# The ratio of group A's two softmax sums: from ScalarE and VectorE to VectorE alone

## The chip, the cores and the metric

The kernel runs on one core of one Trainium2 chip. The metric is the device time of one launch in microseconds. The kernel before has a median of 923.14 us over 3 runs (922.13 to 925.34).

## The reference

Two layers of a transformer trunk work on 512 latent tokens (an 8 x 64 grid) and 256 context tokens, model width 1024. Each layer makes one adaLN-modulated norm, one input projection to 3584 columns, three groups of attention heads (A, B, C), a SiLU gate on each, one output projection and a gated residual. The change lies in group A, differential attention with 4 heads of two softmaxes each:

```python
s = jnp.einsum('bqhmd,bkhmd->bhmqk', q, k).astype(jnp.float32) * (q.shape[-1] ** -0.5)
p = jax.nn.softmax(s, axis=-1)
a = (p[:, :, 0] - lam * p[:, :, 1]).astype(v.dtype)
return jnp.einsum('bhqk,bkhd->bqhd', a, v)
```

Latent queries attend to 512 latent and 256 context keys in one softmax; context queries (in layer 0 only) attend to the 256 context keys. The result of each head is RMS-normalised, so a common factor of a row does not matter much until that norm. Group B is grouped-query attention, group C attention in a neighbourhood of the grid with a bias table.

## The kernel before, in words

**Products.** A projection in float32 is made of three matmuls of rounded parts (high x high, high x low, low x high; lines 679 to 681, tile `proj`). Weights stream in through SyncE's DMA queue (line 76, `raw`); ScalarE casts each piece to its high part (line 89, `whi`) and VectorE or GpSimd makes the low part (line 92, `wlo`). The results leave PSUM tile by tile: norms and rotary embedding for queries and keys (lines 462 to 534, through ScalarE, VectorE and GpSimd, then a transposing DMA), a scaled split for values (lines 585 and 586), a tanh gate (lines 600 to 606).

**Attention.** A unit is 128 queries and one pair of softmaxes in group A (16 latent units in each layer, 8 context units in layer 0), or one head in groups B and C. Five steps follow one another:

- `stage_S`: TensorE makes the scores (line 775, tile `sc`, two PSUM buffers).
- `stage_M`: VectorE takes the row maximum (line 830; in group C line 827 with the bias table), ScalarE turns it into the bias of the exponential (line 832).
- `stage_E`: ScalarE takes the exponential (line 844) into a float32 tile `p` (tag `p32`, three buffers) and, in group A, also its row sum into `dn`. A latent unit of group A does S, M and E twice, once for each softmax.
- `stage_H`: for group A the two exponentials become one matrix, p0 + k p1, where k = -lambda sum0 / sum1 (lines 857 to 860). Then ScalarE casts it to float16 (line 864, tile `hl`), GpSimd (for a few of the units in group C VectorE) subtracts to get the rest (line 865), and a transposing DMA on SyncE's queue brings both into `pt` (line 867).
- `stage_PV`: TensorE multiplies `pt` with the values (lines 900 and 901, tile `pv`), and for every fourth unit of group A `pv_evac` normalises and gates the result (lines 911 to 929).

Step H runs one unit behind the scores, step PV four units behind. Since the tile `p` has three buffers and a latent unit of A uses two, the second exponential of a unit waits until line 860 of the unit before has read the first.

**Stages.** Each layer runs A, then B, then C. Beside the attention of each stage TensorE works through filler: the projections for the next group (during A those of B and a gate, during B those of C and a gate), and during C the output projection (`op` at lines 1087 to 1089; in layer 1 also `oh` and `ot`, lines 1141 to 1143) and the transposes of the attention's result (`yt`, lines 618 and 640). Before group C's first scores a bias table is loaded (line 985, into `stB`, the buffer that held B's queries and keys) and scaled by ScalarE (line 987).

**What sets the order.** The code is written unit by unit, but a scheduler orders the instructions of each engine when the program is built, by priorities and by its own estimates of the durations. So a change of one instruction can move others on every engine, and in later stages. Each engine then works through its own list strictly in that order: an instruction that waits holds up everything behind it on its engine.

**The lines that the change touches.** In `stage_H` line 857 (ScalarE) makes m = -lambda sum0, line 858 (VectorE) makes 1/sum1, line 859 (ScalarE) makes k = m/sum1, and line 860 (VectorE) the combination p0 + k p1 over 128 x 768 (context units 128 x 256). All of m, k and the sums are columns of 128 x 1 in `dn`. There are 40 units, so 40 of each.

Of the kernel before, what the change touches and what calls it, by code (L numbers as in the profile page):

```python
# [15 lines left out]
AF = mybir.ActivationFunctionType  # L16
ALU = mybir.AluOpType
# [99 lines left out]
def tile_hybrid_block(ctx: ExitStack, tc: tile.TileContext, xT_d, cT_d, ng_d, w_ada, bT_d, w_in, w_out,  # L117
# [7 lines left out]
    V, A, G, PE, SP = nc.vector, nc.scalar, nc.gpsimd, nc.tensor, nc.sync  # L125
# [3 lines left out]
    def sb(shape, dt=F32, tag="", bufs=1):  # L129
        return pool.tile(shape, dt, tag=tag, bufs=bufs, name=tag)  # L130
# [169 lines left out]
    lc = {}  # L300
# [547 lines left out]
    def stage_H(l, u, lo_eng):  # L848
        hl = sb([128, 1536], F16, "hl", 4)
        if u["g"] == "A":  # L850
            n, h = u["w"], u["segs"][0] // 2
            den = acc["dn", u["j"]]
            p0 = u["p", 0][:, 0:n]
            p = u["p", 1][:, 0:n] if u["lat"] else u["p", 0][:, n:2 * n]
            k = den[:, 1, 4 + h:5 + h]
            m = den[:, 0, 4 + h:5 + h]
            A.activation(out=m, in_=den[:, 0, h:h + 1], func=AF.Copy, scale=lc[l]["nlam"])
            V.reciprocal(k, den[:, 1, h:h + 1])
            A.activation(out=k, in_=k, func=AF.Copy, scale=m)
            V.scalar_tensor_tensor(out=p, in0=p, scalar=k, in1=p0, op0=ALU.mult, op1=ALU.add)  # L860
        else:
            n = u["w"] * len(u["segs"])
            p = u["p", 0][:, 0:n]
        A.copy(out=hl[:, 0:n], in_=p)  # L864
        lo_eng.tensor_tensor(out=hl[:, n:2 * n], in0=p, in1=hl[:, 0:n], op=ALU.subtract)  # L865
        pt = sb([128, 12, 128], F16, "pt", 4)
        SP.dma_start_transpose(out=pt[:, 0:n // 64, :], in_=hl[:, 0:2 * n])  # L867
        u["pt"] = pt
# [106 lines left out]
    def attn(l, g):  # L975
# [15 lines left out]
        for x in range(n + LAG):  # L991
# [25 lines left out]
            if HLAG <= x < n + HLAG:  # L1017
                stage_H(l, us[x - HLAG], share("H"))
# [341 lines left out]
```

## Time and profile before

| | |
|---|---|
| median of 3 runs | 923.14 us (922.13 to 925.34) |
| profiled execution, its own time | 924.36 us |
| its span in the trace | 922.5 us (1.86 us lie around it) |
| mean granted clock of TensorE | 0.952 |
| stage A of layer 0 (scores of A from 108 us on) | about 112 to 270 us |
| stage A of layer 1 | about 630 to 735 us |
| stage C of layer 1 and the end | about 825 to 922.5 us |

How to read it: the stage limits are taken from where the first and last instructions of a stage start, and stages overlap by a few microseconds. Busy time of an engine in a stretch is the time in which it has an instruction under way; the rest is a wait for another engine, a DMA or its own sequencer. Idle time of an engine other than the one that bounds a stage costs nothing by itself.

### The profile page before, as it was taken

Reading aid. Unit: us, or ns where it says so; the run is one execution under the profiler, and the core shown is the slowest. Engines: PE = TensorE matmul, PEld = TensorE weight load, DVE = VectorE, ACT = ScalarE, POOL = GpSimd, SP = SyncE. Lnnn points to the kernel's source line nnn. Section 1 sums busy time; section 2 is a strip of 40 time slices with the busy share of each in tenths; the row PEclk is TensorE's granted clock in tenths of the full one; section 3 lists DMA queues with packets and bytes.
Section 4 is the critical chain, followed back from the end, with each engine's and each line's share of the span. In section 5 each row is a group of like instructions: output and inputs, shape, how many; then the busy total and the mean of one; then the engine's idle time right before and its main releaser. Section 6 shows DMA issues by size and latency. Waiting matters only on the chain. (4 is left out here: it accounts for less than half of the span.)

```text
span 922.5 us, 17964 instructions
## 1 busy us (share of the span) xinstructions
PE 825.3 (89%) x6386; PEld 706.9 (77%) x6386; DVE 679.0 (74%) x1306; ACT 592.4 (64%) x1269; POOL 541.3 (59%) x502
## 2 busy tenths in 40 slices
PE   5898997996998899897999989989959999988988
PEld 3787876895987789785778889879849878865767
DVE  5985787988678866558656797789877967656843
ACT  5334577784887687477653445478758988839830
POOL 2638855899698565435330047938988886634420
PEclk9899999998999999898999989989969999997989
DMA  9834895645979996998898713784557899996642
GB/s 328 306 97 126 202 214 141 139 95 134 193 162 222 202 223 173 219 259 215 184 211 237 258 52 101 185 185 102 133 128 175 149 190 246 231 260 171 152 91 83
DMA packets 307049, 165.46 MB, mean 179 GB/s; under 512 B 256528, under 2 KB 275216, under 8 KB 306704
## 3 DMA queue, kind: packets, MB, share of 16 engines
q1 hardware_dynamic: 306960, 164.33, 73.7%
q8 instruction: 50, 0.82, 0.4%
q14 instruction: 39, 0.32, 0.1%
HBM read 86.55 MB, written 15.47 MB: 111 GB/s over the span
## 5 line engine op out<-in xcount | busy, mean ns | idle before, releaser
L865 POOL TENSOR_TENSOR hl<-p,hl 128x768 f16<-128x768 f32 (+3 forms) x138 | 203.6, 1480 | 164.9 <-ACT hl L864 148.8
L679 PE MATMUL proj<-whi,bigL 128*128 128x384 f32 (+1 forms) x592 | 203.0, 344 | 8.4 <-DVE tb L602 4.2
L680 PE MATMUL proj<-wlo,bigL 128*128 128x384 f32 (+1 forms) x592 | 199.4, 337 | 0.8 <-POOL wlo L92 0.7
L681 PE MATMUL proj<-whi,bigL 128*128 128x384 f32 (+1 forms) x592 | 197.3, 335 | 0.0
L844 ACT ACTIVATE p<-sc,nb,gsc 128x768 f32<-128x768 f32 (+3 forms) x200 | 166.4, 846 | 10.6 <-DVE p L860 4.7
L830 DVE TENSOR_REDUCE mx<-sc 128x1 f32<-128x768 f32 (+2 forms) x128 | 118.7, 932 | 33.2 <-PE sc L775 33.0
L679 PEld LDWEIGHTS proj<-whi,bigL 128*128 128x128 f32 x592 | 115.2, 195 | 18.7 <-DVE tb L602 5.9
L864 ACT CAST hl<-p 128x768 f16<-128x768 f32 (+3 forms) x144 | 104.1, 726 | 38.5 <-DMA pt<-hl 22.5
L680 PEld LDWEIGHTS proj<-wlo,bigL 128*128 128x128 f32 x592 | 115.5, 195 | 3.9 <-POOL wlo L92 1.5
L681 PEld LDWEIGHTS proj<-whi,bigL 128*128 128x128 f32 x592 | 114.6, 194 | 2.8 <-issue 2.0
L92 POOL TENSOR_TENSOR wlo<-raw,whi 128x768 fp32r<-128x768 f32 (+1 forms) x44 | 83.4, 1902 | 40.3 <-ACT whi L89 37.5
L89 ACT CAST whi<-raw 128x768 fp32r<-128x768 f32 (+1 forms) x104 | 80.3, 780 | 28.4 <-DMA raw<-in_w_in_dram 14.0
L900 PEld LDWEIGHTS <-pt 128*128 128x128 f16 x736 | 65.5, 99 | 35.3 <-DMA pt<-hl 20.9
L679 PE MATMUL proj<-whi,bigC 128*128 128x384 f32 (+2 forms) x224 | 76.0, 339 | 1.0 <-ACT xn L462 1.0
L92 DVE TENSOR_TENSOR wlo<-raw,whi 128x768 fp32r<-128x768 f32 (+1 forms) x60 | 64.9, 1085 | 15.9 <-ACT whi L89 14.4
L680 PE MATMUL proj<-wlo,bigC 128*128 128x384 f32 (+2 forms) x224 | 74.8, 334 | 0.0
L163 POOL TENSOR_TENSOR rsqb<-rsqb,half 128x12 f32<-128x12 f32 (+2 forms) x25 | 68.4, 2737 | 10.0 <-DVE rsqb L162 9.2
L681 PE MATMUL proj<-whi,bigC 128*128 128x384 f32 (+2 forms) x224 | 74.1, 333 | 0.0
L901 PEld LDWEIGHTS <-pt 128*128 128x128 f16 x736 | 66.0, 100 | 4.3 <-issue 2.2
L832 ACT ACTIVATE nb<-mx,lnp,gsc 128x1 f32<-128x1 f32 (+1 forms) x104 | 39.7, 386 | 36.5 <-DVE mx L830 24.4
L775 PE MATMUL sc<-bigL 128*128 128x512 f16 (+4 forms) x184 | 46.4, 312 | 18.0 <-ACT p L844 17.2
L900 PE MATMUL pv<-vA,pt 128*128 128x128 f16 (+2 forms) x424 | 51.3, 228 | 9.6 <-DMA pt<-hl 9.2
(320 smaller groups left out, 2031.5 us busy)
## 6 DMA issues: line engine op xcount, KB each, us to landing
raw<-in_w_in_dram SPq DMA_DIRECT2D x64, 384.0 KB, 4.0
adw<-in_w_ada_dram SPq DMA_DIRECT2D x68, 256.0 KB, 3.6
raw<-in_w_out_dram SPq DMA_DIRECT2D x16, 384.0 KB, 4.7
raw<-in_w_in_dram SPq DMA_DIRECT2D x16, 256.0 KB, 3.1
g_d<-tb SPq DMA_DIRECT2D x20, 192.0 KB, 2.7
gt<-g_d SPq DMA_DIRECT2D x18, 192.0 KB, 3.4
hl<-in_w_ada_dram SPq DMA_DIRECT2D x12, 256.0 KB, 5.2
pt<-in_w_ada_dram SPq DMA_DIRECT2D x12, 256.0 KB, 5.2
```

The costliest lines, as they stand in the source:

```text
L89: self.nc.scalar.copy(out=hi, in_=raw2)
L92: self.share("W").tensor_tensor(out=lo, in0=raw2, in1=hi.bitcast(F32), op=ALU.subtract)
L163: G.tensor_tensor(out=y, in0=x, in1=half[:, 0:n], op=ALU.pow)
L679: PE.matmul(ps, lhsT=xh, rhs=hi, start=(kt == 0), stop=False)
L680: PE.matmul(ps, lhsT=xh, rhs=lo, start=False, stop=False)
L681: PE.matmul(ps, lhsT=xl, rhs=hi, start=False, stop=(kt == KT - 1))
L830: V.tensor_reduce(out=mx[:, 0:ns], in_=ps[:, 0:w * ns].rearrange("p (a b) -> p a b", b=w), axis=AX.X, op=ALU.max)
L844: A.activation(out=p[:, w * x:w * x + w], in_=u["ps", i][:, w * x:w * x + w], func=AF.Exp, bias=u["nb", i][:, x:x + 1], scale=lc[l]["sc"][ ...
L864: A.copy(out=hl[:, 0:n], in_=p)
L865: lo_eng.tensor_tensor(out=hl[:, n:2 * n], in0=p, in1=hl[:, 0:n], op=ALU.subtract)
L900: PE.matmul(po[r, :], lhsT=pt[:, b, r], rhs=V_[:, vt, c0:129], start=first, stop=False)
L901: PE.matmul(po[r, 0:65 - c0], lhsT=pt[:, nb + b, r], rhs=V_[:, vt, c0:65], start=False, stop=stop)
```

## The change

The ratio is made by VectorE alone: the reciprocal of the second sum as before, and then one product of two factors, (1/sum1) x (-lambda) x sum0, in one instruction. ScalarE's two instructions for each unit go, and the column m is no longer written.

```diff
             k = den[:, 1, 4 + h:5 + h]
-            m = den[:, 0, 4 + h:5 + h]
-            A.activation(out=m, in_=den[:, 0, h:h + 1], func=AF.Copy, scale=lc[l]["nlam"])
             V.reciprocal(k, den[:, 1, h:h + 1])
-            A.activation(out=k, in_=k, func=AF.Copy, scale=m)
+            V.scalar_tensor_tensor(out=k, in0=k, scalar=lc[l]["nlam"], in1=den[:, 0, h:h + 1], op0=ALU.mult,
+                                   op1=ALU.mult)
             V.scalar_tensor_tensor(out=p, in0=p, scalar=k, in1=p0, op0=ALU.mult, op1=ALU.add)
```

In the changed kernel the lines from the reciprocal on have numbers one lower: the reciprocal is line 856, the new product 857 and the combination 859, the cast 863, the bias table's load 984.

The scheduler makes a new order from this. On VectorE, for the first unit of stage A in layer 0, the old order has two other instructions between the reciprocal and the combination:

```order
206 L246 COPY adt<-ada 128x128
207 L858 RECIPROCAL dn<-dn 128x1
208 L506 TENSOR_TENSOR stg<-xn,stg 128x16x32
209 L830 TENSOR_REDUCE mx<-sc 128x1
210 L860 SCALAR_TENSOR_TENSOR p_1679<-p_1679,dn,p_1669 128x768
211 L602 SCALAR_TENSOR_TENSOR tb<-sq,proj 128x256
```

In the new order, at the same place on VectorE, the reciprocal, the new product (`dn<-dn,lm`) and the combination stand together:

```order
206 L246 COPY adt<-ada 128x128
207 L856 RECIPROCAL dn<-dn 128x1
208 L857 SCALAR_TENSOR_TENSOR dn<-dn,lm 128x1
209 L859 SCALAR_TENSOR_TENSOR p_1679<-p_1679,dn,p_1669 128x768
210 L506 TENSOR_TENSOR stg<-xn,stg 128x16x32
211 L830 TENSOR_REDUCE mx<-sc 128x1
```

So the combination moved ahead of a split for the keys (line 506) and ahead of the next row maximum (line 830). On ScalarE, at the same unit, the old order is:

```order
103 L832 ACTIVATE nb<-mx,lm,gsc 128x1
104 L857 ACTIVATE dn<-dn,lm 128x1
105 L844 ACTIVATE p_1679,dn<-sc,nb,gsc 128x768
106 L505 CAST stg<-xn 128x16x32
107 L859 ACTIVATE dn<-dn 128x1
108 L600 ACTIVATE sq<-proj 128x256
109 L832 ACTIVATE nb<-mx,lm,gsc 128x1
110 L844 ACTIVATE p_1706,dn<-sc,nb,gsc 128x768
111 L864 CAST hl<-p_1679 128x768
```

and the new one:

```order
103 L832 ACTIVATE nb<-mx,lm,gsc 128x1
104 L844 ACTIVATE p_1679,dn<-sc,nb,gsc 128x768
105 L505 CAST stg<-xn 128x16x32
106 L600 ACTIVATE sq<-proj 128x256
107 L863 CAST hl<-p_1679 128x768
108 L832 ACTIVATE nb<-mx,lm,gsc 128x1
109 L844 ACTIVATE p_1706,dn<-sc,nb,gsc 128x768
```

Here the cast of the combined matrix moved ahead of the next unit's exponential. Later stages change as well. On SyncE's queue in layer 1, around the load of group C's bias table (`stB<-in_btab_dram`), the old order is:

```order
411 L867 DMA_TRANSPOSE pt<-hl 128x12x128
412 L606 DMA g_d_82<-tb 128x384
413 L867 DMA_TRANSPOSE pt<-hl 128x12x128
414 L606 DMA g_d_82<-tb 128x384
415 L867 DMA_TRANSPOSE pt<-hl 128x12x128
416 L606 DMA g_d_82<-tb 128x384
417 L985 DMA stB<-in_btab_dram 128x2944
418 L76 DMA raw<-in_w_out_dram 128x512
```

and the new one:

```order
394 L971 DMA gt<-g_d_82 128x384
395 L866 DMA_TRANSPOSE pt<-hl 128x12x128 x2
396 L1098 DMA bigC<-x_d 128x1024
397 L866 DMA_TRANSPOSE pt<-hl 128x12x128
398 L984 DMA stB<-in_btab_dram 128x2944
399 L866 DMA_TRANSPOSE pt<-hl 128x12x128
400 L638 DMA xn<-o_d_80 128x256 x3
```

The table's load now stands ahead of B's last transposing DMA and no longer behind three stores of gates (line 606). Counted over TensorE's whole order, the products of filler (matmuls of `proj`, `op`, `oh`, `ot`) that stand between the scores are these:

| filler products on TensorE | before | changed |
|---|---|---|
| layer 0, first to last score of A | 610 | 634 |
| layer 1, first to last score of A | 489 | 434 |
| layer 1, B's last score to C's first score | 18 | 75 |
| layer 1, C's first to last score | 173 | 97 |
| layer 1, behind the last score | 151 | 209 |

## The prediction

> **What bounds the kernel now.** I read the engines' busy shares first, then the busy time by stage, then the waits in the two A stages, and last the groups by line. The page's shares:
>
> ```profile
> PE 825.3 (89%) x6386; PEld 706.9 (77%) x6386; DVE 679.0 (74%) x1306; ACT 592.4 (64%) x1269; POOL 541.3 (59%) x502
> ```
>
> TensorE (PE) is busy for 825.3 of 922.5 us, and the change takes no work from it. It can only pay where TensorE is idle, 97 us in all. The busy time by stage, for the two A stages (columns: stretch, length, then busy us of PE, PEld, DVE, ACT, POOL, the granted clock, DMA share, GB/s):
>
> ```profile
> 112.00:270.00 158.00, 139.17 (x1080) 121.81 (x1079) 133.32 (x221) 121.92 (x308) 122.54 (x126) 0.97 0.69 155
> 630.00:735.00 105.00, 91.39 (x633) 81.78 (x632) 89.61 (x122) 82.53 (x182) 92.25 (x82) 0.92 0.61 136
> ```
>
> TensorE idles 158.0 - 139.2 = 18.8 us and 105.0 - 91.4 = 13.6 us there, 32.4 us together. No engine is far ahead: VectorE (DVE) has 84% and 85%, ScalarE (ACT) 77% and 79%, GpSimd (POOL) 78% and 88%. What TensorE waits for, first in 112 to 270, then in 630 to 735 us (total, times, longest):
>
> ```profile
> PE sc L775 <- ACT p L844: 10.0, 6, 3.3
> PE pv L900 <- DMA pt<-hl: 3.8, 5, 1.9
> ...
> PE sc L775 <- ACT p L844: 5.2, 3, 3.9
> PE pv L900 <- DMA pt<-hl: 4.6, 2, 3.0
> ```
>
> Scores wait for an exponential to free their PSUM buffer for 10.0 + 5.2 = 15.2 us, and the value products for the transposed matrix for 8.4 us. Both hang on the chain exponential, ratio, combination, cast, transposing DMA, so the ratio lies on a path that TensorE waits for, some of the time. Its instructions and their neighbours, by group (count | busy us, mean ns | idle before and releaser):
>
> ```profile
> L844 ACT ACTIVATE p<-sc,nb,gsc 128x768 f32<-128x768 f32 x112 | 110.8, 989 | 8.8 <-DVE p L860 4.5 <-DVE vnb L546 0.9 <-POOL hl L865 0.4
> L864 ACT CAST hl<-p 128x768 f16<-128x768 f32 x88 | 72.9, 829 | 18.5 <-DVE p L860 14.9 <-DMA pt<-hl 3.0
> L832 ACT ACTIVATE nb<-mx,lm,gsc 128x1 f32<-128x1 f32 x64 | 24.5, 383 | 17.9 <-DVE mx L830 17.4
> L844 ACT ACTIVATION_READ_ACCUMULATOR p<-sc,nb,gsc 128x1 f32 x80 | 15.5, 193 | 0.0
> L857 ACT ACTIVATE dn<-dn,lm 128x1 f32<-128x1 f32 x40 | 11.7, 292 | 0.1
> L859 ACT ACTIVATE dn<-dn 128x1 f32<-128x1 f32 x40 | 11.7, 291 | 7.5 <-DVE dn L858 7.3
> L858 DVE RECIPROCAL dn<-dn 128x1 f32<-128x1 f32 x40 | 6.3, 157 | 11.1 <-ACT p L844 11.0
> L860 DVE SCALAR_TENSOR_TENSOR p<-p,dn,p 128x768 f32<-128x768 f32 x32 | 43.5, 1360 | 3.1 <-ACT dn L859 3.0
> ```
>
> The reader should see that ScalarE waits for VectorE here at least as much as the other way: 17.4 us for row maxima, 14.9 us for the combination, 7.3 us for the reciprocal.
>
> **The change part by part.** A difference under 0.3% (2.8 us) is about what a measurement of this kernel cannot tell from none.
>
> (a) *Two ScalarE instructions less in each unit.* ScalarE loses 40 x (292 + 291 ns) = 23.3 us of work. A latent unit costs it now 2 x (383 + 989 + 193) + 829 + 292 + 291 = 4542 ns, so 12.8% go. If the scores' wait for exponentials shrinks in that proportion, TensorE gains 0.128 x 15.2 = 1.9 us. Besides, line 859 no longer stands in ScalarE's order waiting for the reciprocal, in 112 to 270 and in 630 to 735 us:
>
> ```profile
> ACT dn L859 <- DVE dn L858: 2.4, 4, 1.5
> ...
> ACT dn L859 <- DVE dn L858: 4.7, 4, 3.5
> ```
>
> That is 7.1 us in which the exponentials and casts queued behind it stood still. What is late next is the cast at line 864, which waits for the combination, so I take half, 3.6 us. Term: -5.5 us; bounds 0 (ScalarE then waits for VectorE instead) and -15.2 (all the waits for exponentials).
>
> (b) *One VectorE product more in each unit.* It has 128 x 1 elements and two tensor inputs in SBUF. The trace has no such instruction at this place. Nearest rows from below: the reciprocal, 157 ns. From above, another 128 x 1 product of two SBUF columns (line 365, min/median/max ns):
>
> ```profile
> L365 DVE TENSOR_TENSOR lm<-lm x2: 434/990/1545, 36.6 to 309.0; 128x1 f32<-128x1 f32 x2
> L860 DVE SCALAR_TENSOR_TENSOR p<-p,dn,p x32: 1002/1046/2687, 117.3 to 724.6; 128x768 f32<-128x768 f32 x32
> ```
>
> So a column product with two SBUF inputs can last 1.5 us, and the combination, also with two SBUF inputs, lasts 1.00 us at least but 1.36 us on average, beside a GpSimd that is busy for 78 to 88% of these stages. I add this mean stretch of 358 ns to the reciprocal's 157: 0.515 us each, 20.6 us for 40. Against it stands VectorE's idle time before line 860, which goes:
>
> ```profile
> DVE p L860 <- ACT dn L859: 0.8, 1, 0.8
> ...
> DVE p L860 <- ACT dn L859: 2.3, 4, 0.7
> ```
>
> That leaves 20.6 - 3.1 = 17.5 us more on VectorE. It counts only where VectorE is full:
>
> ```profile
> 156.00:192.00 36.00, 32.72 (x251) 29.37 (x250) 34.44 (x50) 27.29 (x70) 33.27 (x39) 1.00 0.54 119
> 204.00:216.00 12.00, 9.31 (x59) 7.84 (x57) 11.68 (x11) 5.50 (x13) 12.00 (x10) 1.00 0.54 81
> 638.00:650.00 12.00, 11.96 (x77) 11.25 (x78) 11.96 (x16) 9.23 (x23) 10.85 (x10) 1.00 0.67 157
> 662.00:674.00 12.00, 8.49 (x56) 7.25 (x55) 11.39 (x12) 9.52 (x23) 12.00 (x8) 0.96 0.58 147
> ```
>
> In these 72 of 263 us VectorE is busy for 69.5, and in two of the four stretches TensorE idles over 2 us. So 72/263 = 0.27 of the 17.5 us arrive: +4.7 us. Bounds by the reciprocal (6.3 - 3.1) x 0.27 = +0.9, by line 365 (39.6 - 3.1) x 0.27 = +9.9. The product adds no wait on another engine: the reciprocal ahead of it waits for the second exponential already. Queued behind it are the combination and the next row maximum, for which ScalarE waits.
>
> The Trainium skill, "Perfetto Trace Analysis", section Optimizing Scalar/DVE Operations, says that a saturated VectorE may be relieved by giving work to ScalarE, which speaks against this change. By that rule alone all of the 17.5 us would be added; the rows agree with its condition in the four stretches only.
>
> (c) *Two stalls near the end.* The new order moves more than the ratio. In layer 1 TensorE stands at the passage from B to C, and once more behind the last scores:
>
> ```profile
> 825.00:840.00 15.00, 6.86 (x25) 4.42 (x22) 7.65 (x19) 10.53 (x21) 1.54 (x2) 0.55 0.68 232
> 885.00:895.00 10.00, 6.08 (x64) 4.35 (x64) 4.54 (x9) 3.54 (x9) 3.65 (x4) 0.82 0.81 135
> ```
>
> 8.1 and 3.9 us of idle time. The cause of the first, from SyncE's queue, the chain that ended last, and the waits:
>
> ```profile
> 821.95 0.52 SPq L606 DMA_DIRECT2D g_d<-tb  x1
> 822.52 0.45 SPq L985 DMA_DIRECT2D stB<-in_btab_dram  x1
> ...
> 822.52 7.69 DMA stB<-in_btab_dram
> ...
> ACT stB L987 <- DMA stB<-in_btab_dram: 4.3, 1, 4.3
> ```
>
> The bias table is issued behind three gate stores, takes 7.69 us, and ScalarE waits for it with TensorE's evacuations queued behind. In the new order the load stands ahead of those stores and 75 filler products, not 18, lie between B's last score and C's first. Behind the last score stand 209 products, not 151, which cover the second stall. I take three quarters of 12.0: -9.0 us; bounds 0 and -12.0.
>
> (d) *Less cover in stage A of layer 1.* 55 filler products fewer stand there (489 to 434). One step of them, by two rows of TensorE's timeline:
>
> ```profile
> 660.07 0.34 PE L681 MATMUL proj<-whi,bigL 128*128 128x384 f32 x1
> 660.25 0.34 PE L679 MATMUL proj<-whi,bigL 128*128 128x384 f32 x1
> ```
>
> 55 x 0.17 us = 9.4 us less cover. ScalarE's 16 units there lose 16 x 0.583 = 9.3 us of work, so most of it is matched; because VectorE is full I charge a third: +3.1 us; bounds 0 and +9.4.
>
> (e) *Less cover in stage C of layer 1.* 76 products fewer (173 to 97), each with a step of 0.23 us:
>
> ```profile
> 875.20 0.40 PE L1087 MATMUL op<-bigL,whi 128*128 128x512 f32 x1
> 875.43 0.39 PE L1088 MATMUL op<-bigL,whi 128*128 128x512 f32 x1
> ...
> 840.00:885.00 45.00, 45.00 (x329) 32.66 (x328) 33.59 (x74) 34.77 (x70) 18.91 (x17) 1.00 0.62 135
> ```
>
> TensorE is full in these 45 us; without 76 x 0.23 = 17.5 us it needs 27.5, but ScalarE's work there is 34.8. So up to 7.3 us of waiting come back if ScalarE runs without a gap: +5.0 us taken; bounds 0 and +17.5.
>
> (f) Layer 0 changes too: 24 products more beside A. Its sign is open: 0, with 24 x 0.17 = 4.1 us to both sides.
>
> Sum: -5.5 + 4.7 - 9.0 + 3.1 + 5.0 = -1.7 us. On the profiled execution's 924.36 us that is 922.7; it is 1.22 us above the median of 923.14, so the median becomes 921.4 us.
>
> **The rivals.**
>
> *The relief arrives.* (a) with the whole of the 7.1 us, -9.0; the product costs what the reciprocal does, +0.9; stage A needs no more cover, (d) 0; (c) and (e) as above: -9.0 + 0.9 - 9.0 + 5.0 = -12.1, 911.0 us. For it speaks that the combination follows the reciprocal at once in the new order; against it that ScalarE waits 14.9 us for the combination and not for itself.
>
> *VectorE becomes the bound of stage A (slower).* The product waits behind GpSimd's instructions, at 990 ns as line 365 does: (b) +9.9. Then the chain is no shorter and the missing cover shows in full: (d) +9.4. With the rest, -5.5 + 9.9 - 9.0 + 9.4 + 5.0 = +9.8, 932.9 us. Its place is 630 to 735 us, where GpSimd has 92.25 of 105 us. With (d) in full, it decides by over 2.8 us once (b) is above 2.9, a product of 0.35 us on average. For it speaks the combination's 2687 ns; against it that half of the combinations keep to 1046 ns.
>
> The Trainium skill, "SBUF — State Buffer", section Who interferes with whom, states the mechanism: a VectorE instruction with two SBUF inputs contends with a GpSimd instruction that reads SBUF, and the loser is blocked. The spread of line 860, 1002 to 2687 ns, agrees.
>
> *Nothing arrives.* The ratio is hidden, and what the order gives at one place it takes at another: 923.1 us.
>
> **How the numbers follow.** The sum, with its own range of 917 to 926 us by the two signs of (f): 0.43, of which 0.25 lies within 0.3%, 0.11 below and 0.07 above. The relief arrives: 0.26. VectorE becomes the bound: 0.26. Nothing arrives: 0.05. So faster 0.11 + 0.26 = 0.37, within 0.3% 0.25 + 0.05 = 0.30, slower 0.07 + 0.26 = 0.33. The range takes in the two outer cases with about two microseconds beyond each, 909 to 934 us, and leaves out a wider spread of (e) or (f).
>
> **What would show it.** Right: lines 857 and 859 gone from ScalarE, its busy time about 569 us; 40 products on VectorE of about 0.5 us and no wait of the combination for ScalarE; TensorE's idle time at the passage from B to C below 4 us, and above 13.6 us in layer 1's stage A. Wrong: products that last 0.16 us (then the first rival), or near 1 us with TensorE idle over 20 us in layer 1's stage A (then the second); or a difference that sits in layer 0 behind stage A, which the sum holds at nothing.

## The result and the profile after

The changed kernel has a median of 934.27 us over 8 runs (926.52 to 939.63), the kernel before 922.83 us over 8 runs beside them (921.34 to 926.50). The ratio is 1.0116, 95% interval 1.0088 to 1.0144: slower by 11.4 us, where I forecast a gain of 1.7. The profiled execution of the changed kernel took 931.33 us (span 929.5), 7.0 us more than that of before, so the profile shows about three fifths of the loss; a second profile, below, shows it again.

The engines' shares on the page:

```profile
PE 829.0 (89%) x6386; PEld 708.9 (76%) x6386; DVE 687.3 (74%) x1346; ACT 577.2 (62%) x1189; POOL 543.7 (58%) x502
```

ScalarE has 15.2 us less and VectorE 8.3 us more; both go the way that the edit says. TensorE's idle time went from 97.2 to 100.5 us, and its busy time rose by 3.7 us with the same 6386 matmuls. The two A stages in the windows of the prediction (same columns as there):

```profile
112.00:270.00 158.00, 143.34 (x1089) 126.05 (x1088) 131.71 (x244) 114.11 (x260) 122.26 (x124) 0.96 0.69 154
630.00:735.00 105.00, 86.86 (x598) 75.08 (x598) 86.13 (x127) 75.22 (x152) 93.34 (x83) 0.92 0.63 139
```

Layer 0 idles 14.7 us instead of 18.8, layer 1 18.1 instead of 13.6. What TensorE waits for, in the same two windows:

```profile
PE sc L775 <- ACT p L844: 6.8, 4, 3.0
PE pv L899 <- DMA pt<-hl: 5.3, 5, 2.1
...
PE sc L775 <- ACT p L844: 10.9, 7, 4.5
PE pv L899 <- DMA pt<-hl: 3.2, 4, 1.3
```

The scores' wait for exponentials fell by 3.2 us in layer 0 and rose by 5.7 us in layer 1. The groups, with the idle time of the engine ahead of them, and what ended it, behind the second bar:

```profile
L844 ACT ACTIVATE p<-sc,nb,gsc 128x768 f32<-128x768 f32 x112 | 110.7, 989 | 21.2 <-DVE p L859 14.8 <-POOL hl L864 1.9 <-DVE vnb L546 0.9
L863 ACT CAST hl<-p 128x768 f16<-128x768 f32 x88 | 72.7, 829 | 22.8 <-DMA pt<-hl 11.8 <-DVE p L859 10.4
L859 DVE SCALAR_TENSOR_TENSOR p<-p,dn,p 128x768 f32<-128x768 f32 x32 | 39.7, 1240 | 0.6
L832 ACT ACTIVATE nb<-mx,lm,gsc 128x1 f32<-128x1 f32 x64 | 24.6, 384 | 23.8 <-DVE mx L830 23.6
L857 DVE SCALAR_TENSOR_TENSOR dn<-dn,lm 128x1 f32<-128x1 f32 x40 | 18.6, 464 | 1.1
L856 DVE RECIPROCAL dn<-dn 128x1 f32<-128x1 f32 x40 | 6.2, 155 | 16.6 <-ACT p L844 16.5
```

The product takes 464 ns on average (I had 515), and the combination no longer waits for ScalarE. But ScalarE's idle time ahead of the 768-wide exponentials rose from 8.8 to 21.2 us and ahead of the biases (line 832) from 17.9 to 23.8: it stands still for longer than the 15.2 us of busy time that it lost. Most of the first rise is waiting for the combination (`DVE p L859`), 14.8 us where it was 4.5.

**Where the loss sits.** I cut layer 1 at its scores: first to last score of A, of B, the passage from B to C, first to last score of C, the end. Before:

```profile
599.50:719.60 120.10, 103.56 (x732) 92.10 (x732) 99.98 (x152) 92.74 (x216) 95.15 (x93) 0.90 0.59 140
722.80:803.90 81.10, 77.85 (x639) 67.04 (x639) 59.84 (x89) 69.17 (x115) 60.24 (x41) 1.00 1.03 218
803.90:807.90 4.00, 4.00 (x32) 3.59 (x29) 2.71 (x6) 3.88 (x8) 3.62 (x3) 1.00 0.71 145
807.90:881.80 73.90, 65.03 (x460) 48.70 (x456) 48.75 (x98) 49.72 (x96) 27.40 (x22) 0.91 0.75 183
881.80:922.50 40.70, 32.31 (x258) 29.36 (x257) 16.54 (x39) 6.89 (x17) 3.65 (x4) 0.87 0.39 94
```

and in the changed kernel:

```profile
598.30:714.50 116.20, 94.05 (x677) 81.65 (x677) 96.13 (x160) 81.60 (x175) 89.15 (x88) 0.91 0.63 144
718.90:802.80 83.90, 79.08 (x604) 68.00 (x604) 60.38 (x87) 66.50 (x109) 62.43 (x43) 0.98 0.88 192
802.80:820.40 17.60, 16.46 (x129) 15.08 (x129) 14.10 (x19) 13.92 (x24) 12.40 (x6) 1.00 0.92 269
820.40:882.00 61.60, 50.14 (x370) 36.49 (x370) 40.12 (x87) 40.33 (x82) 23.37 (x19) 0.86 0.82 174
882.00:929.50 47.50, 43.03 (x318) 38.06 (x318) 22.68 (x47) 11.53 (x25) 5.11 (x5) 0.97 0.35 92
```

Layer 1's first score of A starts 1.2 us earlier (598.3 against 599.5); the end comes 7.0 us later. Stage A has 55 matmuls less in the trace (677 against 732) and is only 3.9 us shorter. B with the passages on both sides is 17.6 us longer (3.2 + 81.1 + 4.0 before, 4.4 + 83.9 + 17.6 after), mostly at the passage to C with its 97 matmuls more. C has 90 less and is 12.3 us shorter; the end has 60 more and is 6.8 us longer: -3.9 + 17.6 - 12.3 + 6.8 - 1.2 = 7.0. So the last score of C comes at the same time (881.8 and 882.0 us), and in this pair of profiles what was moved behind it is the loss.

The 1.2 us ahead of layer 1 are not the change's: in a second profile of the changed kernel, below, stage A begins at 593.7 us. From the first score of A to the end, layer 1 takes 922.5 - 599.5 = 323.0 us before and 929.5 - 598.3 = 331.2 us in the changed kernel, and 929.8 - 593.7 = 336.1 us in its second profile. These losses of 8.2 and 13.1 us lie on either side of the medians' 11.4.

### The profile page after: what moved, and what is told of

Same layout as the page of the kernel before. It is cut to its first block, busy times and chain, and to the rows that moved or that the text cites. A ratio compares the mean times of both kernels' runs of the same rounds, so it can differ in the third digit from the quotient of the medians.

```text
span 929.5 us, 17901 instructions
## 1 busy us (share of the span) xinstructions
PE 829.0 (89%) x6386; PEld 708.9 (76%) x6386; DVE 687.3 (74%) x1346; ACT 577.2 (62%) x1189; POOL 543.7 (58%) x502
## 5 line engine op out<-in xcount | busy, mean ns | idle before, releaser
L864 POOL TENSOR_TENSOR hl<-p,hl 128x768 f16<-128x768 f32 (+3 forms) x138 | 206.6, 1501 | 170.6 <-ACT hl L863 161.5
L679 PE MATMUL proj<-whi,bigL 128*128 128x384 f32 (+1 forms) x592 | 206.5, 349 | 8.9 <-DVE tb L602 3.5
L680 PE MATMUL proj<-wlo,bigL 128*128 128x384 f32 (+1 forms) x592 | 201.7, 341 | 2.2 <-DVE wlo L92 2.2
L681 PE MATMUL proj<-whi,bigL 128*128 128x384 f32 (+1 forms) x592 | 199.1, 338 | 0.0
L844 ACT ACTIVATE p<-sc,nb,gsc 128x768 f32<-128x768 f32 (+3 forms) x200 | 166.2, 845 | 25.6 <-DVE p L859 14.8
L679 PEld LDWEIGHTS proj<-whi,bigL 128*128 128x128 f32 x592 | 117.0, 198 | 18.9 <-DVE tb L602 5.4
L681 PEld LDWEIGHTS proj<-whi,bigL 128*128 128x128 f32 x592 | 116.1, 197 | 3.3 <-issue 1.6
L899 PEld LDWEIGHTS <-pt 128*128 128x128 f16 x736 | 66.4, 100 | 37.2 <-DMA pt<-hl 21.2
L679 PE MATMUL proj<-whi,bigC 128*128 128x384 f32 (+2 forms) x224 | 74.5, 333 | 0.4 <-ACT xn L462 0.4
L681 PE MATMUL proj<-whi,bigC 128*128 128x384 f32 (+2 forms) x224 | 72.9, 328 | 0.0
L92 DVE TENSOR_TENSOR wlo<-raw,whi 128x768 fp32r<-128x768 f32 (+1 forms) x60 | 61.9, 1034 | 11.6 <-ACT whi L89 9.6
L900 PEld LDWEIGHTS <-pt 128*128 128x128 f16 x736 | 67.0, 100 | 2.8 <-issue 0.8
L899 PE MATMUL pv<-vA,pt 128*128 128x128 f16 (+2 forms) x424 | 52.0, 229 | 10.8 <-DMA pt<-hl 10.6
L775 PEld LDWEIGHTS <-bigL 128*128 128x128 f16 (+2 forms) x344 | 24.5, 101 | 43.7 <-issue 35.6
```

The source lines that it names most:

```text
L92: self.share("W").tensor_tensor(out=lo, in0=raw2, in1=hi.bitcast(F32), op=ALU.subtract)
L679: PE.matmul(ps, lhsT=xh, rhs=hi, start=(kt == 0), stop=False)
L680: PE.matmul(ps, lhsT=xh, rhs=lo, start=False, stop=False)
L681: PE.matmul(ps, lhsT=xl, rhs=hi, start=False, stop=(kt == KT - 1))
L775: PE.matmul(ps, lhsT=q, rhs=k, start=n == 0, stop=n == b[2] - 1)
L844: A.activation(out=p[:, w * x:w * x + w], in_=u["ps", i][:, w * x:w * x + w], func=AF.Exp, bias=u["nb", i][:, x:x + 1], scale=lc[l]["sc"][ ...
```

## The experiments

Three theories. **O**: the new order of the lists costs the time, not the operations. **V**: the product on VectorE costs it, above all its long ones. **F**, from the windows above: filler taken out of a stage saves nothing where the attention's chain bounds the stage, and costs where it is put. The other letters are explained in the expectations that use them.

To hold an order fixed, a kernel gets a table with each engine's instructions in the wanted order, and every instruction is tied to the one before it in the table without a semaphore. The table is made from the order of one of the two kernels, and its numbers are left out of the diff:

```diff
+    pin_order(tc)
...
+ORDER = (
...
+        if prev is not None:
+            tc.add_manual_dep(ins[at], ins[prev].name, dep, reason="order")
```

**The changed kernel again** (no edit).

> The changed kernel once more, for a second profile and more times. Its eight times fell into two groups, 926.5 to 931.3 and 937.2 to 939.6 us; the profiled execution (931.33) is of the lower one. Theory O (the new order of the lists costs the time) and theory V (the product on VectorE costs it) both expect a median of 930 to 938 us, TensorE idle about 100 us in all, and the last score of group C at about 882 us as in the kernel before. If the upper group is a matter of the granted clock, a profile from it has the same idle time and a lower clock (0.94 in place of 0.951); if it is a matter of waits, it has 6 us or more of further idle time at one place.

Measured 935.18 us (931.55 to 937.78; before 925.00), ratio 1.0105 (1.0073 to 1.0137). The profile (931.55 us) idles in stage A of layer 1 as the first one does (22.3 us for 22.1), and its end is the same:

```profile
593.70:712.20 118.50, 96.21 (x675) 83.19 (x676) 95.75 (x160) 81.72 (x175) 88.98 (x87) 0.90 0.63 141
882.10:929.80 47.70, 43.16 (x319) 38.16 (x318) 22.68 (x47) 11.54 (x25) 5.11 (x5) 0.99 0.35 93
```

Longer runs go with a lower mean clock: over these six, 0.951 at 932.06 and 0.938 at 937.78 us. Both profiles of this kernel fell on runs below 932 us, so where the few microseconds above them go is not shown by these two; the run with one tensor input, below, comes nearer to it.

**New operations in the old order** (the changed kernel with the table of the kernel before; the product right behind its reciprocal).

> The changed operations (reciprocal and product on VectorE, nothing on ScalarE) in the order of the kernel before on every engine; the product stands right behind the reciprocal, the two ScalarE instructions are simply left out of their list. Theory O (the new order costs the time): 918 to 925 us, that is no slower than before, since 23.4 us of ScalarE's work are gone and the fillers stand where they stood (173 products beside the scores of group C in layer 1, 151 behind the last). Theory V (the product, 464 ns on average and up to 1890 ns, costs it on VectorE): 930 to 938 us, with more idle time of TensorE in the two A stages (layer 1: 15.5 us before, 21.2 in the changed kernel).

Measured 928.47 us, ratio 1.0052 (1.0028 to 1.0075): half of the changed kernel's loss, but not none. Both theories missed, O with 925 us at most and V with 930 at least. The product is even longer there:

```profile
L857 DVE SCALAR_TENSOR_TENSOR dn<-dn,lm 128x1 f32<-128x1 f32 x40 | 21.9, 547 | 1.4
```

**Old operations in the new order** (the kernel before with the table of the changed one; line 857 ahead of the second exponential, line 859 one instruction behind it).

> The operations of the kernel before (two ScalarE instructions for each unit, no product) in the order of the changed kernel on every engine; the first of the two stands ahead of the second exponential, the second one instruction behind it, ahead of the cast. Theory O: 931 to 942 us, as slow as the changed kernel or slower, since the fillers stand where the new order has them (97 products beside the scores of group C in layer 1, 209 behind the last) and ScalarE has its 23.4 us again. Theory V: 920 to 926 us, as the kernel before.

Measured 936.90 us, ratio 1.0138 (1.0106 to 1.0170). The old operations are as slow as the new ones once they stand in the new order: as theory O forecast, and against V. By itself this run does not part the order from a misfit, since the old operations stand here in an order that was made for others. The pair that parts them comes below: the same operations with a short product, in the new order (the next run) and in the old one.

**The product with one tensor input**, new order.

```diff
-            V.scalar_tensor_tensor(out=k, in0=k, scalar=lc[l]["nlam"], in1=den[:, 0, h:h + 1], op0=ALU.mult,
-                                   op1=ALU.mult)
+            V.tensor_scalar(out=k, in0=k, scalar1=lc[l]["nlam"], scalar2=den[:, 0, h:h + 1], op0=ALU.mult,
+                            op1=ALU.mult)
```

> The changed kernel in its own order, but the product takes the reciprocal as its only tensor and both factors (minus lambda, the first sum) as columns of scalars, so that the instruction has one tensor input in SBUF instead of two. Theory V with contention as its cause (product 224 ns at the median, but 464 on average, because it waits for GpSimd): the product falls to about 0.2 us, 40 x 0.26 = 10.6 us of VectorE's work go, and the time falls by 3 to 10 us against the changed kernel, to 924 to 931. Theory O: the product may fall as well, but the time stays within 3 us of the changed kernel.

Measured 935.72 us, ratio 1.0114 (1.0083 to 1.0145), the same as the changed kernel. The product lost its long ones (min/median/max), first the changed kernel, then this one:

```profile
L857 DVE SCALAR_TENSOR_TENSOR dn<-dn,lm x40: 200/224/1890, 115.0 to 720.1; 128x1 f32<-128x1 f32 x40
```

```profile
L857 DVE TENSOR_SCALAR dn<-dn,lm x40: 256/273/277, 114.7 to 723.7; 128x1 f32<-128x1 f32 x40
```

The average fell from 464 to 273 ns, and in this order that was worth nothing. The profiled execution took 937.34 us, so it is one of the longer ones, in the order of the changed kernel:

```profile
PE 833.7 (89%) x6386; PEld 712.0 (76%) x6386; DVE 684.4 (73%) x1346; ACT 578.8 (62%) x1189; POOL 547.8 (59%) x502
```

Its span is 935.2 us, so TensorE idles for 101.5 us (100.5 in the first profile of the changed kernel) and is busy for 833.7 us (829.0), at a mean granted clock of 0.942 (0.951). So of the 5.7 us more, 4.7 are the same matmuls taking longer; no new wait of that size stands behind them.

**Which part of the order.** In the projections of layer 1 both orders have done exactly the same instructions, and at the start of its stage C all but eight, so a table can be put together of parts. All three kernels have the new operations; the rest of each is the old order.

> The changed operations; layer 0 in the changed kernel's order, from the projections of layer 1 on in the order of the kernel before (at the seam both orders have done exactly the same instructions). Theory L (the new order loses in layer 1's stages A and B, and nowhere else): 0.995 to 1.005 of the kernel before, as the changed operations in the old order throughout (1.005) or a little faster. Theory S (the loss is spread over the whole program, or comes from the clock): half of it, about 1.008 or more.

Measured 929.59 us (before 923.86), ratio 1.0057 (1.0030 to 1.0083), as with the old order throughout: layer 0's new order gives and takes nothing.

> The changed operations; the order of the kernel before everywhere except in layer 1 from its projections to the start of stage C, where the changed kernel's order stands. Between these seams the profiles have 208.4 us before and 222.1 and 226.4 us in the changed kernel, up to the first score of C, with about 25 products more done by then (some 5 us). Theory L: 1.010 to 1.018 of the kernel before, as slow as the changed kernel or slower. Theory T (the products that the new order leaves behind the last score cost it, 209 in place of 151): no slower than the changed operations in the old order, 1.002 to 1.008.

Measured 933.51 us, ratio 1.0106 (1.0070 to 1.0141): within theory L's range and above theory T's.

> The changed operations; the order of the kernel before up to the start of layer 1's stage C, and from there to the end that of the changed kernel (97 filler products beside the scores, 209 behind the last). Theory T (the end costs it): 1.009 or more of the kernel before. Theory L: 0.996 to 1.006; the two stalls of the old order's end are exchanged for waits of the same size.

Measured 934.81 us, ratio 1.0121 (1.0093 to 1.0148). Here theory L, as I put it, falls, and theory T fell with the run before: the new order costs in C as well as in A and B, about 0.5% and 0.7% on top of the 1.0052, and both halves together cost no more than one. A likely reason is that the order of C was made to follow that of A and B. Without it, TensorE stands longer in stage C than in either parent (8.9 and 11.5 us of idle time); the window, and what TensorE waits for in it:

```profile
809.60:884.30 74.70, 56.17 (x397) 41.19 (x395) 43.99 (x90) 46.77 (x93) 28.64 (x23) 0.86 0.79 177
```

```profile
PE proj L679 <- DVE tb L602: 8.5, 2, 7.2
```

74.7 - 56.2 = 18.5 us of idle time, 8.5 of them for a gate that no filler covers.

**Row maximum first** (new order; on VectorE, in layer 1's stage A, 14 row maxima moved ahead of the combination).

> The changed kernel's own order, but for VectorE in stage A of layer 1: of 14 units the next row maximum, which stands behind the combination, is moved ahead of it (11 of them ahead of the reciprocal too). Theory Q (in the new order VectorE stands at the reciprocal until the second exponential is done, 12.2 us against 5.4 before, with the next row maximum queued behind it, for which ScalarE and then TensorE wait): VectorE's wait there falls to 6 us or less, TensorE's wait for exponentials in layer 1 from 11.4 to 7 us or less, and the time by 4 to 8 us against the changed kernel, to 1.003 to 1.008 of the kernel before. Theory F (55 filler products fewer stand beside the stage, and the order on VectorE is not what makes it wait): within 3 us of the changed kernel, 1.008 to 1.014.

Measured 942.48 us, ratio 1.0215 (1.0178 to 1.0253): slower still. Theory Q falls, and theory F's range (1.008 to 1.014) is missed too. VectorE's waits in that stage, first in the changed kernel, then here:

```profile
DVE dn L856 <- ACT p L844: 12.2, 8, 3.0
...
DVE mx L830 <- PE sc L775: 1.2, 2, 0.7
```

```profile
DVE mx L830 <- PE sc L775: 16.7, 9, 5.7
DVE dn L856 <- ACT p L844: 5.3, 4, 3.3
```

The wait at the reciprocal fell as foreseen, and a longer one for scores took its place, probably because the scores wait for the exponentials in their turn. So a shorter wait at the reciprocal does not by itself shorten the stage; the place of the row maximum does matter, since this one costs about 1% more.

**Filler left out.** Kernel before, its own order, 50 products left out at one place, every other list as it was; the projection is less exact for it.

```diff
-        PE.matmul(ps, lhsT=xh, rhs=lo, start=False, stop=False)
+        left_out() or PE.matmul(ps, lhsT=xh, rhs=lo, start=False, stop=False)
...
-            PE.matmul(ps[:, 0:w], lhsT=wh, rhs=yl, start=False, stop=False)
+            left_out() or PE.matmul(ps[:, 0:w], lhsT=wh, rhs=yl, start=False, stop=False)
```

> The kernel before, its order unchanged, but 50 of the 489 filler products that stand between the first and the last score of group A in layer 1 are left out (high input by low weights; every third candidate), so that the projection there is less exact. At a step of 0.17 us they are 8.5 us of TensorE. Theory F (the attention's chain bounds this stage, so that filler taken out of it leaves TensorE waiting): 0 to 3.5 us less than before, 0.996 to 1.000, and TensorE's idle time in the stage up by 5 us or more from 16.5. Theory P (TensorE bounds it, and the new order's loss comes from the lists of the other engines): 6 to 8.5 us less, 0.991 to 0.994.

Measured 928.17 us (before 924.36), ratio 1.0046 (1.0027 to 1.0064): with less work the kernel is slower. Its stage A:

```profile
596.90:717.20 120.30, 97.50 (x682) 84.54 (x682) 98.84 (x152) 91.03 (x214) 94.49 (x93) 0.90 0.62 140
```

120.3 us, as before (120.1), with 22.8 us of idle time for 16.5. The stage does not shorten at all, and its idle time grows by 6.3 us, as theory F said. F's time (0.996 to 1.000) is missed, because the rest of the program got longer.

> The same for stage C of layer 1: 50 of the 173 filler products between its first and its last score are left out. At a step of 0.23 us they are 11.5 us of TensorE. Theory F: 0 to 5 us less than before, 0.995 to 1.000, with the waits of TensorE between 840 and 882 us growing from nothing. Theory P: 8 to 11.5 us less, 0.988 to 0.991.

Measured 916.88 us, ratio 0.9920 (0.9892 to 0.9948), 7.5 us less, between the two theories. C is 5.8 us shorter for 8.8 us less of TensorE:

```profile
806.60:874.70 68.10, 56.21 (x407) 40.58 (x403) 49.22 (x98) 49.85 (x99) 28.63 (x23) 0.87 0.86 201
```

> The same for the end: 50 of the 151 filler products behind the last score of layer 1 are left out. Both theories: close to their full time, 50 x 0.2 = 10 us less, 7 to 11 us, 0.988 to 0.993, since nothing but TensorE's products and their evacuation is left there. If much less comes off, the end too is bounded by something else (the stores of the result), and the 58 products that the new order put there are not what costs.

Measured 919.59 us, ratio 0.9959 (0.9941 to 0.9978), 4.8 us less, half of what both theories expected. The end is 4.6 us shorter for 6.0 us less of TensorE: a product there costs 0.12 us and not 0.2, and 1.4 us come back as idle time. At 0.12 us the 58 products that the new order put there are an estimated 7.0 us, near the 6.8 by which the end grew.

```profile
884.30:920.40 36.10, 26.28 (x210) 22.38 (x209) 16.26 (x39) 7.09 (x18) 3.65 (x4) 0.84 0.45 106
```

**The bias table earlier** (kernel before, own order; one instruction of SyncE's list moved).

> The kernel before with its own operations and order, but group C's bias table in layer 1 is loaded earlier: its load stands behind the store that was issued at 808.5 us, ahead of three stores of gates and four groups of transposing DMAs, where it was issued at 822.5. This is the first half of term (c) by itself. If the term is right (the 8.1 us of idle time at 825 to 840 us hang on this load, and nothing else is late there): 5 to 8 us less than before, 0.991 to 0.995. If the stall only passes to the next late thing (the transposed matrices of the last units of B, or gates that now wait behind the table), or the other work of stage C has no use for the time: within 2 us of before, 0.998 to 1.002.

Measured 920.74 us (before 925.05), ratio 0.9959 (0.9941 to 0.9977): half of the 8.1 us, and faster than both kernels. SyncE issued the load at 806.0 us:

```profile
806.03 0.38 SPq L985 DMA_DIRECT2D stB<-in_btab_dram  x1
```

The stretches of 10 us at that place, first in the kernel before, then here:

```profile
820.00:830.00 10.00, 6.49 (x62) 5.33 (x58) 5.66 (x10) 3.17 (x6) 1.98 (x1) 0.83 1.04 300
830.00:840.00 10.00, 5.13 (x16) 3.33 (x16) 5.42 (x13) 9.76 (x19) 1.54 (x2) 0.50 0.55 187
```

```profile
820.00:830.00 10.00, 5.65 (x48) 4.16 (x47) 8.27 (x19) 8.72 (x17) 1.26 (x1) 0.76 0.93 249
830.00:840.00 10.00, 10.00 (x71) 7.01 (x71) 5.04 (x12) 8.89 (x18) 5.71 (x5) 0.90 0.67 140
```

TensorE waits in one of the two stretches where it waited in both.

**One tensor input in the old order; the same with the table earlier; no product at all.** The first two are the edits above, together in the second; the third takes out the product's line, so that the combination takes 1/sum1 alone and minus lambda and the first sum are left out of the result.

> The changed operations in the old order, with the product in its form with one tensor input (273 ns each, without the long ones). Theory V2 (what is left of the loss in the old order, 1.0052, is the long products: 14.9 us more of VectorE than before): 0.997 to 1.002, and VectorE's busy time down by some 7 us against the form with two tensors (693.9). Theory O2 (the old order fits the old operations, and the product's length does not matter): 1.003 to 1.008, as with two tensors.

> Old order, the product with one tensor input, and the bias table's load moved ahead as in the run with the kernel before. If both gains are real and independent, 0.988 to 0.997 of the kernel before, the sum of the two runs; if the table gains nothing, the same as the product's form alone.

> Old order without the product: the combination takes the reciprocal of the second sum alone, so that minus lambda and the first sum are left out of the computation. ScalarE has the 23.4 us less, VectorE nothing more: the outer limit of what relief of ScalarE can bring in this order. Theory R (relief arrives, and the product eats it): 0.990 to 0.997. Theory N (ScalarE's relief is worth nothing in an order made for the old operations): 0.998 to 1.004.

Measured 925.96, 922.31 and 929.22 us (before 925.05), ratios 1.0010 (0.9992 to 1.0029), 0.9979 (0.9961 to 0.9997) and 1.0044 (1.0024 to 1.0065). The first supports V2: in the old order the long products cost about 0.4%. The third speaks against it: with no product at all the time is as long as with the long one. So the 0.4% do not follow the product's length, and what decides it stays open. The table moved ahead takes 0.3% off the first (1.0010 to 0.9979), about what it took off the kernel before, though the run's own range (0.988 to 0.997) is missed by a little. One thing is clear from the first and the third: ScalarE's relief by 23 us of instructions brought no gain in the old order either.

The first is also the pair to the run with one tensor input in the new order. The operations are the same, no product is long, and only the order differs: 1.0010 (0.9992 to 1.0029) in the old order, 1.0114 (1.0083 to 1.0145) in the new. So the order alone is worth about 1%, nearly the whole loss. This is the strongest evidence for theory O.

## Why the prediction was wrong, by its own steps

**The step that failed** is the premise that less work on ScalarE shortens stage A. It stands in (d), with its sentence that ScalarE's units lose 9.3 us of work, "so most of it is matched", and in (a), which takes 5.5 us of gain for the same work. ScalarE's work does not set the length of layer 1's stage A, so nothing was matched. The run with no product shows it, in the old order with the same filler (the kernel before: 120.1 us, ScalarE busy for 92.74):

```profile
597.90:718.60 120.70, 103.15 (x732) 91.72 (x732) 99.35 (x153) 87.05 (x186) 94.40 (x92) 0.92 0.61 140
```

ScalarE is busy for 5.7 us less, VectorE has no product more, and the stage is no shorter. In (d) I charged a third of 9.4 us. In the profiled pair 55 products less shorten the stage by 3.9 us and leave 5.6 us more of idle time; where 50 were left out by themselves, nothing was saved. So the term was between 5.6 and the whole 9.4, the slower rival's price for it. This part of the pair repeats: the five profiles with stage A in the new order (VectorE's list as the scheduler made it) idle there for 20.3 to 23.8 us, the ten with it in the old order and all its products for 16.5 to 19.8.

What may hold the stage was in the windows of before, and I did not read it; after the length, the columns are those of the prediction.

```profile
666.00:676.00 10.00, 5.06 (x35) 3.63 (x33) 8.24 (x11) 8.29 (x20) 10.00 (x7) 0.85 0.52 140
676.00:686.00 10.00, 4.14 (x23) 3.22 (x22) 6.70 (x7) 4.27 (x9) 10.00 (x9) 0.50 0.52 130
```

GpSimd has no gap for 20 us while TensorE idles for 10.8 of them. In the changed kernel it has none there either:

```profile
666.00:676.00 10.00, 6.54 (x44) 5.23 (x43) 7.96 (x10) 6.42 (x13) 10.00 (x7) 1.00 0.73 178
676.00:686.00 10.00, 2.87 (x19) 1.42 (x17) 6.67 (x8) 5.65 (x12) 10.00 (x9) 0.57 0.43 98
```

ScalarE's exponentials wait in these 20 us, first before, then in the changed kernel:

```profile
ACT p L844 <- DVE p L860: 0.6, 1, 0.6
ACT p L844 <- POOL hl L865: 0.4, 1, 0.4
```

```profile
ACT p L844 <- DVE p L859: 4.6, 2, 2.5
ACT p L844 <- POOL hl L864: 1.9, 1, 1.9
```

So what they wait for first is the combination on VectorE, and GpSimd's subtraction second. Whether the full GpSimd stands behind both is not shown: no run took work from it.

**(a), -5.5 taken, nothing arrived.** Line 859's wait went, but ScalarE's waits for row maxima and combinations took its place, and TensorE's wait for exponentials in the two A stages went from 15.2 to 17.7 us (6.8 + 10.9). The runs in the old order with short products and with none (1.0010 and 1.0044) show no gain of this work either.

**(b), +4.7 taken.** The size was near (464 ns for 515). Its effect was not: nothing in the new order, and up to 0.4% in the old one, with the contradiction named above. One reading in it was wrong too: TensorE idles over 2 us in three of the four stretches (3.3, 2.7 and 3.5 us), not in two; the term does not use this.

**(c), -9.0 taken.** Right in part. The second stall shrank from 8.4 to 4.5 us in the end's window. The first went from its place, but stage C still idles for 11.5 us (8.9 before), now at 832 to 862:

```profile
832.00:842.00 10.00, 5.22 (x54) 3.83 (x52) 6.63 (x17) 8.12 (x18) 5.14 (x5) 0.97 1.16 227
842.00:852.00 10.00, 7.73 (x69) 5.81 (x69) 6.17 (x13) 8.08 (x18) 4.48 (x4) 0.67 1.07 249
852.00:862.00 10.00, 6.85 (x29) 4.39 (x27) 7.49 (x15) 5.92 (x13) 6.15 (x5) 0.51 0.41 100
```

By itself the table's load was worth 4.3 us (925.05 - 920.74), not 8.1 x 0.75 = 6.1.

**(e), +5.0 taken.** Fifty products out of C saved 7.5 us where their steps are 11.5, so 76 lose 17.5 x (1 - 7.5 / 11.5) = 6.1 us of cover: the term was about right by itself. (c) and (e) together were to give -4.0 us; the idle time of C and the end went from 17.3 to 16.0 us, -1.3.

**(f), 0.** Right: layer 0's new order alone moved nothing (1.0057 against 1.0052).

**The sum in the trace.** Idle time: stage A of layer 1 +5.6 (22.1 - 16.5), C and the end -1.3, B with its passages +2.6 (4.8 + 1.1 - 3.3), layer 0 and the start -3.6, together +3.3; TensorE's longer busy time +3.7. That makes the 7.0 us of the profiled pair. The forecast was -1.7, so 8.7 us are to be accounted for. Stage A has 3.3 of them (5.6 against (a), (b) and (d) together, +2.3), C and the end 2.7 (-1.3 against -4.0). For B with its passages (+2.6) and for TensorE's busy time (+3.7) the prediction had no term, and layer 0 gives 3.6 back.

The busy time and layer 0 are not clearly the change's. The start of layer 1's stage A differs by 4.6 us between two profiles of the changed kernel, and the busy time of the same 6386 matmuls goes from 823.0 us (the table earlier) to 831.3 (new operations in the old order) among profiles in the old order.

Most of the signs that the prediction named for being right came: ScalarE's busy time down (to 577.2 us, for about 569 forecast), products of about 0.5 us, no wait of the combination for ScalarE, idle time at the passage to C below 4 us (1.1), and above 13.6 us in layer 1's stage A (18.1). They could not tell the sum from a loss, because none of them looked at whether stage A got shorter. The slower rival gave 932.9 us, near the median of 934.27, but for another reason: it wanted products near 1 us, and the run with one tensor input shows that their length did not matter in this order.

## What to carry to other kernels

Where a scheduler makes the order, an edit of one instruction is two changes, and the order can weigh more than the operations: pin one order under both sets of operations before judging either. Filler that leaves a stage saves its full time only if TensorE bounds that stage; leave some of it out by experiment and see whether the stage shortens. A single load moved ahead in one queue gained 4.3 us here, more than the 1.7 that the edit was to gain.

## What the runs showed of the hardware

**TensorE's clock falls behind a stretch of waiting, and stays low.** In the rows at 666 to 686 us the granted clock goes to 0.50 in the second ten, with TensorE busy for 4.14 us in it; in the changed kernel at 832 to 862 it goes from 0.97 to 0.67 and then 0.51, and the same score products (128 x 256, line 775, on `bigL`) take 271, 334 and 429 ns on average in these three stretches. So a stall costs more than its idle time. The Trainium skill, "TensorE: Matmul & The Clock Gate", Part 1, says that the array is gated to half its clock after an idle window of about 3.4 us; these rows agree with the half, and show it held for a stretch of ten microseconds in which TensorE works now and then.

**With a second tensor input in SBUF a 128 x 1 product lasted up to 1890 ns**; with the same factors as scalar columns (and `tensor_scalar` in place of `scalar_tensor_tensor`) it took 256 to 277 ns, in the same order and beside the same work. That the long ones go with the second input agrees with what the prediction cites from the Trainium skill, "SBUF — State Buffer", section Who interferes with whom: an instruction with two SBUF inputs contends with GpSimd's reads.

**ScalarE's short instructions overlap with the next.** The 80 instructions taken away had 23.4 us of duration, but its busy time fell by 15.2. In ScalarE's timeline of before the next instruction starts before the short one has ended:

```profile
834.30 0.39 ACT L832 ACTIVATE nb<-mx,lnp,gsc 128x1 f32<-128x1 f32 x1
834.59 0.47 ACT L622 CAST bigL<-yt 128x384 fp32r<-128x384 f32 x1
```

834.30 + 0.39 = 834.69, 0.10 us behind the next one's start; 80 such overlaps would be an estimated 8 us, which is what is missing.

**Less work can be slower.** Fifty products less in stage A cost 0.46%; its profile shows the idle time (97.2 to 102.0 us in all), but not why layer 1 behind stage A, with unchanged lists, took 207.6 us in place of 202.9. The mean granted clock of its twelve runs is 0.948, that of the kernel before beside them 0.952. That stays open.
